# A diagonal of a 2-D prefix sum: another first load, and the corner loaded with the last batch

## Chip, cores and metric

One core of one Trainium2 chip. The metric is the device time of one execution in microseconds (us), lowest is best. Most executions of one kernel lie within 0.3% of each other.

## The reference

```python
x = randn(4, 4224, 4224)              # float32, 285.47 MB
ps = cumsum(cumsum(x, axis=1), axis=2)
diag = diagonal(ps, axis1=1, axis2=2)
return cumsum(diag, axis=1)            # (4, 4224)
```

Every element of x counts somewhere, so all of it has to be read once. For each batch the kernel sums row pieces and column pieces, and from these builds the increments of the diagonal.

## The kernel before

GpSimd's software queue loads x in strips of 768 or 384 rows and casts them to bf16 on the way, three strips ahead. VectorE, ScalarE and TensorE sum each strip. In the last batch, the last rows are split: *part a* (256 rows) and *part b* (128 rows, whose columns lie in four quarters), so that little is left to do after the last byte. One piece, the *head*, is fetched by the SP queue at the very start, while GpSimd still prepares its first descriptors.

```python
HC = 528
src_a = x[LB, T0:TB, :].rearrange("(h p) w -> p h w", p=P)
head = last.tile([P, 2, HC], FP32, name="head")
nc.sync.dma_start(out=head, in_=src_a[:, :, N - HC : N])      # corner of part a
...
for i in range(NBUF):                                          # first strips
    t = strip_tile()
    load_rows(t, 0, i * F2 * P)                                # nc.gpsimd.dma_start
...
row_sums(hs[:, 0:2], head)                                     # at the start
for h in range(2):
    masked(hmu[:, h, :w], head[:, h, HC - w : HC], um1[:, :w], hu[:, h : h + 1])
...
# last batch, after its strips: part a, then the quarters of part b
for sb, c0, c1 in ((0, 0, CB), (1, 0, CB), (2, 0, CB), (3, 0, bcut), (3, bcut, CB)):
    nc.gpsimd.dma_start(out=part_b[:, sb, c0:c1], in_=...)
...
row_sums(arows, asum)                                          # totals of part a
weigh(arows[:, 0:1], weights, 0, start=True)                   # matmuls into fin (PSUM)
weigh(arows[:, 1:2], weights, P)
weigh(ones_col, by, M0)                                        # by: quarter 0 of part b
weigh(dtot, weights, M0)
for k, ca in ((0, 512), (1, 448)):
    act_sum(bsum[:, k, 0:1], part_b[:, k + 1, :ca])
    pair_sum(bsum[:, k, 1:2], part_b[:, k + 1, ca:])
    if k == 1:
        finish(0, M0)                                          # yl = fin + c12
    row_sums(btot[:, k : k + 1], bsum[:, k])
    weigh(btot[:, k : k + 1], weights4, M0 + (k + 1) * R)
... # esum of quarter 3, three matmuls into fin_e, finish(M0, GW), ye = fin_e + yl
```

## Time and profile before

| | before |
|---|---|
| median of the first three runs | 668.09 us |
| median of the six runs beside the changed kernel | 668.83 us (667.1 to 669.88) |
| span of the profiled execution | 665.7 us |
| busy: DMA engines / VectorE / TensorE / ScalarE | all but the ends / 50% / 31% / 21% |

### The profile page before, as it was taken

How to read it: one execution, taken by the hardware profiler on the slowest of the kernel's cores; microseconds unless marked ns; L12 is line 12 of the kernel's file. 1: busy time of each engine (PE TensorE's matmuls, PEld its weight loads, DVE VectorE, ACT ScalarE, POOL GpSimd, SP SyncE). 2: the span in 40 equal slices, each digit the busy share in tenths (PEclk: the TensorE clock that was granted, in tenths of full speed). 3: DMA queues.
4: the chain of work that ended last, by engine and by line, in shares of the span. 5: the costliest groups of instructions: out<-in, count | busy, mean ns of one | idle time of the engine just before them, and what ended most of it. 6: DMA issues, size and time to landing. Idle time of an engine off the chain costs nothing.

```text
span 665.7 us, 2561 instructions
## 1 busy us (share of the span) xinstructions
PE 204.8 (31%) x979; PEld 98.2 (15%) x979; DVE 334.6 (50%) x166; ACT 140.3 (21%) x226; POOL 32.0 (5%) x61
## 2 busy tenths in 40 slices
PE   0081522403117143130221623404032264250427
PEld 0030211101003021110110311202011031120103
DVE  3161625456916153454782524436288333352867
ACT  0001121406300103040630020304063002030436
POOL 7000000000000000000000000000000000001000
PEclk9995857656558585675755957666565586766758
DMA  9999999999999999999999999999999999999998
GB/s 203 219 219 219 219 218 218 219 209 212 219 221 218 218 218 219 218 218 216 209 218 220 218 216 218 219 218 218 218 213 215 219 217 215 219 217 218 218 205 161
DMA packets 7670, 143.23 MB, mean 215 GB/s; under 512 B 702, under 2 KB 1002, under 8 KB 2154
## 3 DMA queue, kind: packets, MB, share of 16 engines
q0 software_dynamic: 7296, 142.47, 99.9%
q1 hardware_dynamic: 362, 0.61, 0.3%
q8 instruction: 7, 0.11, 0.1%
q14 instruction: 5, 0.04, 0.0%
HBM read 285.47 MB, written 0.07 MB: 429 GB/s over the span
## 4 chain that ended last, share of the span: by engine, by line
DVE 47%; another core or an unknown queue 44%; DMA 5%; PE 2%; issue 1%; DVEq 0%; POOLq 0%
DVE acc L239 29%; DVE mu L329 8%; DVE strip L330 8%; DMA strip<-in_x_dram 5%; PE d L213 1%; DVE c L445 1%; PE fold L213 1%; DVE pu L239 0%; PE fin L213 0%; DVE c L259 0%; DVE rows L369 0%; DVE acc L344 0%; PE carry_ps L213 0%; DVE carry L443 0%
## 5 line engine op out<-in xcount | busy, mean ns | idle before, releaser
L213 PE MATMUL d<-strip,sel 128*11 128x384 bf16 x603 | 138.6, 403 | 359.9 <-DMA strip<-in_x_dram 359.9
L234 ACT ACTIVATE dump<-strip 128x416 bf16<-128x416 bf16 (+8 forms) x112 | 128.4, 1146 | 521.9 <-DMA strip<-in_x_dram 519.2
L329 DVE TENSOR_TENSOR mu<-strip,um 128x4608 bf16<-128x4608 bf16 (+1 forms) x24 | 52.4, 2183 | 305.8 <-DMA strip<-in_x_dram 305.7
L239 DVE TENSOR_REDUCE acc<-strip 128x6 f32<-128x4608 bf16 (+6 forms) x23 | 196.0, 8523 | 0.8
L213 PEld LDWEIGHTS <-sel 128*11 128x11 bf16 x849 | 86.2, 102 | 504.7 <-issue 463.0
L213 PE MATMUL d<-mu,sel 128*11 128x384 bf16 x243 | 49.1, 355 | 45.8 <-DVE mu L329 45.8
L330 DVE TENSOR_TENSOR strip<-strip,mu 128x4608 bf16<-128x4608 bf16 (+1 forms) x24 | 52.4, 2183 | 1.0
L76 POOL DMA_DIRECT2D strip<-in_x_dram x24 | 16.5, 688 | 542.1 <-DVE acc L239 281.5
L234 ACT ACTIVATION_READ_ACCUMULATOR dump<-strip 128x1 f32 x112 | 20.9, 186 | 0.0
L213 PE MATMUL d<-ident,rows 128*11 128x128 f32 x24 | 5.2, 380 | 16.7 <-DVE rows L378 16.7
L213 PE MATMUL fold<-strip,ident_h 128*128 128x480 bf16 x8 | 3.4, 598 | 10.6 <-DMA strip<-in_x_dram 10.6
L213 PE MATMUL fold<-weights,quarter 32*128 32x128 f32 x2 | 0.8, 496 | 17.2 <-POOL quarter L199 17.2
L213 PE MATMUL d<-halves,rows 128*11 128x64 f32 x48 | 5.6, 299 | 0.0
L94 DVE MEMSET um<- 128x4608 bf16 (+1 forms) x2 | 4.9, 2458 | 1.1 <-issue 1.1
L213 PEld LDWEIGHTS d<-halves,rows 128*11 128x11 f32 x48 | 5.1, 136 | 1.5 <-issue 1.5
L213 PEld LDWEIGHTS d<-ident,rows 128*11 128x11 f32 x24 | 2.6, 120 | 18.4 <-DVE rows L378 17.5
L95 POOL TENSOR_SCALAR_AFFINE_SELECT um<-um 128x4608 bf16<-128x4608 bf16 (+1 forms) x2 | 5.2, 2608 | 2.4 <-DVE um L94 2.4
L239 DVE TENSOR_REDUCE pu<-d 11x1 f32<-11x384 f32 x4 | 2.2, 546 | 5.2 <-PE d L213 5.2
L445 DVE TENSOR_TENSOR_SCAN c<-ones_row,carry,c 11x384 f32<-11x384 f32 x4 | 4.0, 1006 | 0.1
L445 DVE TENSOR_TENSOR_SCAN c<-ones_row,carry,d 11x384 f32<-11x384 f32 x4 | 4.0, 1000 | 0.1
L418 POOL DMA_DIRECT2D strip<-in_x_dram x5 | 2.7, 548 | 26.4 <-DMA strip<-in_x_dram 26.4
L213 PEld LDWEIGHTS <-ident_h 128*128 128x128 bf16 x14 | 1.6, 119 | 13.8 <-issue 13.5
(90 smaller groups left out, 41.5 us busy)
## 6 DMA issues: line engine op xcount, KB each, us to landing
strip<-in_x_dram POOLq DMA_DIRECT2D x19, 6336.0 KB, 76.5
strip<-in_x_dram POOLq DMA_DIRECT2D x5, 3168.0 KB, 59.7
strip<-in_x_dram POOLq DMA_DIRECT2D x1, 1080.0 KB, 49.9
strip<-in_x_dram POOLq DMA_DIRECT2D x1, 768.0 KB, 52.8
strip<-in_x_dram POOLq DMA_DIRECT2D x3, 256.0 KB, 54.0
head<-in_x_dram SPq DMA_DIRECT2D x1, 528.0 KB, 3.7
strip<-in_x_dram POOLq DMA_DIRECT2D x1, 192.0 KB, 43.2
strip<-in_x_dram POOLq DMA_DIRECT2D x1, 64.0 KB, 28.6
```

Source lines behind the costliest of these rows:

```text
L76: nc.gpsimd.dma_start(out=o, in_=x[b, r0 : r0 + f * P, :].rearrange("(p f) w -> p f w", f=f))
L94: nc.vector.memset(um, 1.0)
L95: nc.gpsimd.affine_select(out=um, in_=um, compare_op=ALU.is_gt, fill=0.0, base=0, pattern=[[-1, f], [1, f * P]], channel_multiplier=-f,)
L213: nc.tensor.matmul(o, lhsT=lhsT, rhs=rhs, start=start, stop=False, skip_group_check=True)
L234: nc.scalar.activation(out=dump[:, :w], in_=src, func=ACT.Copy, accum_out=acc)
L239: nc.vector.reduce_sum(out=acc, in_=src, axis=AX.X)
L329: nc.vector.tensor_mul(out=mu, in0=block, in1=um)
L330: nc.vector.tensor_sub(out=block, in0=block, in1=mu)
L418: nc.gpsimd.dma_start(out=part_b[:, sb, c0:c1], in_=x[b, r0 : r0 + R, :TB].rearrange("r (k c) -> r k c", k=4)[:, :, c0:c1],)
L445: nc.vector.tensor_tensor_scan(out=c12[:, i, :], data0=ones_row, data1=src, initial=carry[:, i : i + 1], op0=ALU.mult, op1=ALU.add,)
```

## The change

The intent: the first load becomes a contiguous block (32 whole rows, the first quarter of part b) in pieces of 4224 B, more pleasant for the DMA engines than 256 scattered pieces of 2112 B. Its sum is one number for each partition, so the product "by" at the end goes away. In return the corner of part a has to be loaded by GpSimd, in the last batch. The diff, cut to its core:

```diff
-    head = last.tile([P, 2, HC], FP32, name="head")
-    nc.sync.dma_start(out=head, in_=src_a[:, :, N - HC : N])
+    head = last.tile([P, N // 4], FP32, name="head")
+    nc.sync.dma_start(
+        out=head, in_=x[LB, TB : TB + R, :].rearrange("r (k c) -> (r k) c", k=4)
+    )
 ...  # weights4 by iota, shift and max instead of a matmul (cut)
-    row_sums(hs[:, 0:2], head)
-    ...                       # masked sums of the head
+    row_sums(htot, head)
 ...
             if not whole and s == 0:      # after the first strip of the last batch
+                corner = last.tile([P, 2, HC], BF16, name="corner")
+                nc.gpsimd.dma_start(out=corner, in_=src_a[:, :, N - HC : N])
             if not whole and s == 1:
+                row_sums(hs[:, 0:2], corner)
+                ...                       # masked sums of the corner
 ...
-                (0, 0, CB),               # first quarter of part b
 ...
-        ... by_ps, by
-        weigh(arows[:, 0:1], weights, 0, start=True)
+        weigh(dtot, weights, M0, start=True)
+        weigh(htot, weights4, M0)
+        weigh(arows[:, 0:1], weights, 0)
         weigh(arows[:, 1:2], weights, P)
-        weigh(ones_col, by, M0)
-        weigh(dtot, weights, M0)
 ...
-            if k == 1:
-                finish(0, M0)
-            row_sums(btot[:, k : k + 1], bsum[:, k])
-            weigh(btot[:, k : k + 1], weights4, M0 + (k + 1) * R)
+        finish(0, M0)
+        for k in range(2):
+            for i in (1, 0):
+                weigh(bsum[:, k, i : i + 1], weights4, M0 + (k + 1) * R)
```

More of the change, by code (lines that the diff above doesn't have):

```diff
@@ L66 @@
     HC = 528
+    R = P // 4
     src_a = x[LB, T0:TB, :].rearrange("(h p) w -> p h w", p=P)
-    head = last.tile([P, 2, HC], FP32, name="head")
-    nc.sync.dma_start(out=head, in_=src_a[:, :, N - HC : N])
+    head = last.tile([P, N // 4], FP32, name="head")
+    nc.sync.dma_start(
+        out=head, in_=x[LB, TB : TB + R, :].rearrange("r (k c) -> (r k) c", k=4)
+    )
     def strip_tile():
@@ L192 @@
     )
-    R = P // 4
-    quarter = consts.tile([R, P], FP32, name="quarter")
-    nc.gpsimd.memset(quarter, 1.0)
-    for base, step in ((0, 1), (3, -1)):
-        nc.gpsimd.affine_select(
-            out=quarter,
-            in_=quarter,
-            compare_op=ALU.is_ge,
-            fill=0.0,
-            base=base,
-            pattern=[[step, P]],
-            channel_multiplier=-4 * step,
-        )
+    steps = consts.tile([P, P], I32, name="steps")
+    nc.gpsimd.iota(steps, pattern=[[4, P]], base=7, channel_multiplier=-1)
+    nc.vector.tensor_single_scalar(
+        out=steps, in_=steps, scalar=2, op=ALU.arith_shift_right
+    )
+    weights4 = consts.tile([P, P], FP32, name="weights4")
+    nc.vector.tensor_scalar_max(out=weights4, in0=steps, scalar1=0.0)
     ident_h = consts.tile([P, P], BF16, name="ident_h")
@@ L215, in matmul @@
         )
-    w4_ps = psum_s.tile([P, P], FP32, name="fold")
-    matmul(w4_ps, quarter, weights[:R, :P], start=True)
-    weights4 = consts.tile([P, P], FP32, name="weights4")
-    nc.vector.tensor_copy(out=weights4, in_=w4_ps)
-    weights4_h = consts.tile([P, P], BF16, name="weights4_h")
-    nc.vector.tensor_copy(out=weights4_h, in_=w4_ps)
-    ones_col = consts.tile([P, 1], FP32, name="ones_col")
-    nc.vector.memset(ones_col, 1.0)
     def fold_in(o, src, c0, c1, w, start=False):
@@ L284 @@
     dtot = last.tile([P, 1], FP32, name="dtot")
+    htot = last.tile([P, 1], FP32, name="htot")
     hs = last.tile([P, 3], FP32, name="hs")
@@ L287 @@
     hmu = last.tile([P, 3, GW], BF16, name="hmu")
-    row_sums(hs[:, 0:2], head)
-    for h in range(2):
-        w = GW - h * P
-        masked(hmu[:, h, :w], head[:, h, HC - w : HC], um1[:, :w], hu[:, h : h + 1])
-    nc.vector.tensor_sub(out=asum[:, :, 0], in0=hs[:, 0:2], in1=hu[:, 0:2])
+    row_sums(htot, head)
     for b in range(B):
@@ L357 @@
                 nc.gpsimd.dma_start(out=diag_b, in_=x[b, TB:N, TB:N])
+                corner = last.tile([P, 2, HC], BF16, name="corner")
+                nc.gpsimd.dma_start(out=corner, in_=src_a[:, :, N - HC : N])
             if not whole and s == 1:
                 row_sums(hs[:, 2:3], diag_b)
+                nc.vector.memset(hs[:R, 2:3], 0.0)
+                row_sums(hs[:, 0:2], corner)
+                for h in range(2):
+                    w = GW - h * P
+                    masked(
+                        hmu[:, h, :w],
+                        corner[:, h, HC - w : HC],
+                        um1[:, :w],
+                        hu[:, h : h + 1],
+                    )
+                nc.vector.tensor_sub(
+                    out=asum[:, :, 0], in0=hs[:, 0:2], in1=hu[:, 0:2]
+                )
                 masked(hmu[:, 2, :P], diag_b, um1[:, :P], hu[:, 2:3])
@@ L485, in finish @@
             )
-        by_ps = psum_s.tile([P, P], FP32, name="fold")
-        for c in range(0, CB, P):
-            matmul(by_ps, part_b[:, 0, c : c + P], weights4_h, start=c == 0)
-        by = last.tile([P, P], FP32, name="by")
-        nc.scalar.copy(out=by, in_=by_ps)
-        weigh(arows[:, 0:1], weights, 0, start=True)
+        weigh(dtot, weights, M0, start=True)
+        weigh(htot, weights4, M0)
+        weigh(arows[:, 0:1], weights, 0)
         weigh(arows[:, 1:2], weights, P)
-        weigh(ones_col, by, M0)
-        weigh(dtot, weights, M0)
         bsum = last.tile([P, 2, 2], FP32, name="bsum")
-        btot = last.tile([P, 2], FP32, name="btot")
         for k, ca in ((0, 512), (1, 448)):
```

## The prediction

> **What bounds the kernel now.** I read the page first, for what the time is made of, then the chain of waits, to see where the transfers stop setting the pace, and then the timeline of the start and of the end.
>
> The page says that the sixteen DMA engines never rest:
>
> ```profile
> DMA  9999999999999999999999999999999999999998
> q0 software_dynamic: 7296, 142.47, 99.9%
> HBM read 285.47 MB, written 0.07 MB: 429 GB/s over the span
> ```
>
> Every slice is at 9, and nearly all of it is the software queue that GpSimd feeds. The input is 4 x 4224 x 4224 x 4 bytes = 285.47 MB, so everything is read once. No engine is near that: VectorE, the busiest, has 50%. A change that reads as many bytes can therefore win or lose only where the DMA engines do not yet run (the first microseconds) and where the time after a landing is still to pay (the last ones). The end of the chain of waits shows how much that is:
>
> ```profile
> 638.16 10.59 another core or an unknown queue
> ...
> 648.80 3.36 PE fold L213 x8
> 652.15 3.58 PE d L213 x24
> ...
> 658.40 1.00 DVE c L445
> 659.41 0.60 DVE asum L239
> ...
> 660.10 0.17 DVE arows L239
> ...
> 660.32 1.85 PE fin L213 x10
> ...
> 662.19 0.04 DVE yl L483
> ...
> 662.53 0.14 DVE btot L239
> ...
> 662.72 0.27 PE fin L213 x2
> ...
> 663.03 0.45 PE fin_e L213 x6
> ...
> 663.50 0.18 DVE ye L522
> ```
>
> The wait of 10.59 us is a wait for data: at 648.8 us the last strip (rows of the last group but one) lands. From there to the last add at 663.68 us the chain never waits for data again. The stream goes on beside it, and the packet records of the trace put the last packet at 662.40 us. So two paths end together: the computing that follows the landing at 648.8, and the landing of the last block. The timeline shows the second one, and what the ten matmuls of the first are:
>
> ```profile
> 660.32 1.24 PE L213 MATMUL fin<-weights,arows 128*1 128x384 f32 x4 [0.79 <-DVE arows L239]
> 661.39 0.38 PE L213 MATMUL fin<-by,ones_col 128*1 128x128 f32 x2
> 661.61 0.38 PE L213 MATMUL fin<-weights,dtot 128*1 128x128 f32 x2
> 661.83 0.33 PE L213 MATMUL fin<-weights,btot 128*1 128x96 f32 x2
> 662.46 0.47 ACT L234 ACTIVATE dump<-strip 128x320 bf16<-128x320 bf16 x1 [0.27 <-DMA strip<-in_x_dram]
> ```
>
> The last block's sum starts at 662.46, ends with its read-out at 663.02, and fin_e starts at 663.03; the other path's last fin matmuls end at 662.99. They meet within 0.05 us. Lengthening either lengthens the kernel.
>
> At the start the load of the head is alone:
>
> ```profile
> 0.82 0.45 SPq L69 DMA_DIRECT2D head<-in_x_dram  x1
> 1.33 2.25 POOL L76 DMA_DIRECT2D strip<-in_x_dram  x3 [0.81 <-POOLq L538]
> ```
>
> In the packet records the head's 256 pieces of 2112 B run from 1.89 to 4.17 us, and the software queue's first packet starts at 3.78 us. Each engine takes its first strip packet within some 10 ns of its last head piece.
>
> **What the Trainium skill says.** "DMA: Bandwidth & Descriptors", section "Queues, rings and completion order": an engine serves its queue rows in turn, a packet at a time. In this trace the pieces of an engine's head are all done before its first strip packet; so either the strips' descriptors came just then, or they stood behind head pieces already fetched. The trace does not decide it, and what a quicker head is worth hangs on it. Same page, "Why small descriptors are slow (HBM only)": a packet has a fixed overhead. The trace agrees and gives its size: 2048 B written took 173 ns, 4320 B 340 ns, 25344 B 1886 ns, which is 22 ns + 0.0735 ns a byte. Most of the 22 ns overlaps with the next packet: in 658 to 660 us, nearly all packets of 2048 B, the engines moved 209 GB/s, against 217 in a steady stretch. Same page, "SWDGE vs HWDGE vs iDMA": only the software path casts; hence the head is fp32 from SP while the corner becomes a bf16 load by GpSimd. "PSUM — Partial Sum Buffer", section "PSUM bank collisions raise a hardware error": PSUM is to be guarded by bank and not by address. The built program agrees: see the third item below.
>
> **The change, part by part.**
>
> 1. *Head.* Both loads have the same 540,672 B: 128 pieces of 4224 B for 256 of 2112 B. Without the start-up, 16 pieces x 86 ns = 1.38 us for each engine become 8 x about 164 ns = 1.31 us (twice 86 less one fixed part of about 8 ns, an estimate). Measured is 1.96 us per engine; the 0.58 us above 1.38 is slow first pieces (up to 916 ns). If that goes with the number of pieces, or a block in one place opens faster than 256 scattered rows, half of it goes: 0.07 + 0.29 = 0.36 us at best, if the strips' descriptors are already there. I count 0.2 us for not knowing.
>
> 2. *Corner instead of the first quarter of part b.* The corner's 256 packets write 1056 B: 0.0735 x 1056 = 78 ns, and about 5 ns that does not overlap, x 256 / 16 = 1.32 us of all engines. The quarter that goes has 128 packets of 2048 B: 156 ns x 128 / 16 = 1.25 us. The stream's end moves by +0.07 us. But the corner is queued behind the first strip of the last batch, and the quarter stood behind all strips and part a. Every landing between moves back by 1.32 us: also the strip at 648.8 on which the long chain hangs.
>
> 3. *The end.* From 648.8 to the end of arows at 660.27 nothing is changed, so arows ends at 660.27 + 1.32 = 661.59. Then come two matmuls of arows (four passes, 1.24 us with their drain) instead of ten passes (1.85 us): the by product is gone, dtot and htot are weighed earlier. They are done at 662.88, and the add into yl runs to about 663.28 (0.41 us at 662.19 before). The four matmuls of bsum now stand behind this add: the program makes the first of them wait for VectorE's 150th completion, which is that add, because both touch one PSUM tile. They start at 663.33. The sums of pairs (btot) and their two waits are gone, but 96-column and 64-column matmuls come twice: by the spacing above (0.22 us for two passes of 128 columns) 2 x 0.16 + 2 x 0.11 = 0.55 us. fin_e starts at 663.88 and takes 0.45; ye starts at about 664.35 instead of 663.50. Sum: **+0.85 us**, of which +1.32 from the later landing and -0.47 from the shorter path after arows. The path by the last block gives only +0.07 and no longer counts.
>
> 4. *Beside other work.* Three DVE operations on the corner move from the start to the second strip of the last batch: 1.2 + 0.55 + 0.42 + 0.16 us, where VectorE next waits 17.04 us for data; costs nothing. The loads there have two strips queued ahead. Making weights4 by iota and shift instead of a matmul ends long before the first strip lands at 34.8 us. ACT loses a copy of 0.27 us, PE eight matmuls of 0.62 us that were hidden.
>
> Net: 0.85 - 0.2 = **+0.65 us**, 0.1%: 668.09 + 0.65 = about 668.7 us.
>
> **The rivals.** (a) *The head's gain is whole or more*: the strips' descriptors wait from about 3 us, and a block in one place starts so fast that 0.8 us are won; then the two cancel, 668.1 or somewhat less. For it speaks that all sixteen engines switch to the strip without a gap. Against: GpSimd begins its issue at 1.33, and I see no record of when descriptors are ready. (b) *The stream sets the end*: if the long chain had slack, only +0.07 and the head's gain count: 667.9. Against it stand the waits of the chain above, which meet within 0.05 us. (c) *Small pieces in mid-stream cost more*: corner packets at the full 22 ns each would be 1.6 us rather than 1.32: 669.0. (d) *GpSimd's queue runs dry* in the last batch, since two loads take completion semaphores in turn: a slice of DMA at less than 9, some microseconds. Against: one part-b load fewer, and each such wait is for a load that landed 25 us or more before the end.
>
> **Range and chances.** The three runs before span 667.1 to 669.24, so the median of three has some 0.7 us of noise; the terms add about 0.5. I take 667.2 to 670.0. Two per cent is 13 us, for which no view has room, short of a surprise in (d): 0.01 for each side.
>
> **What would show it.** Right: in the changed profile the last strip's landing is later by about 1.1 us (1.32 less the head's gain), the last packet moves by less than 0.3 us, the yl add ends near 663.1 and bsum matmuls begin just after it, with a wait on VectorE; the first strip packets begin 0 to 0.4 us earlier. Wrong: the long chain ends where it did, or the strip lands no later, which would mean that I have mis-sized either the corner or the head; or the DMA row drops in the last batch.

## The result, and the profile after

| | before | after |
|---|---|---|
| median of six runs | 668.83 us | 670.37 us (669.97 to 671.68) |
| span of the profiled execution | 665.7 us | 668.8 us |
| last strip lands (start of the work on it) | 648.80 us | 652.14 us |
| last packet of the strips' queue ends | 662.40 us | 664.46 us |
| ye starts | 663.50 us | 666.64 us |

The ratio is 1.0028 (95% interval 1.0012 to 1.0044), some 1.9 us slower. A ratio here is the mean time of one kernel's runs over that of the other's of the same rounds, so it is not quite the ratio of the medians quoted. By the rule of 2% the verdict is "same"; the time was outside my range, and the change cost about three times what I had counted. The two profiles differ by more, 3.1 us: the profiled execution of before was one of its quicker ones (667.37 us).

From the page of the changed kernel:

```profile
DMA  9999999999999999999999999999999999999996
q0 software_dynamic: 7424, 142.48, 99.6%
HBM read 285.49 MB, written 0.07 MB: 427 GB/s over the span
```

The bytes are as predicted (16 KB more read); no slice but the last, which now holds more time without transfers, is below 9. So the queue did not run dry in the last batch. The end of the chain of waits, changed kernel (start, duration, what; "another core or an unknown queue" is the view's name for a wait that it cannot put down to anything, here the one for the strip's data):

```profile
641.49 10.61 another core or an unknown queue
...
652.14 3.36 PE fold L210 x8
655.49 3.68 PE d L210 x24
...
663.54 0.17 DVE arows L227
...
663.76 1.25 PE fin L210 x4
...
665.04 0.42 DVE yl L482
...
665.50 0.73 PE fin L210 x8
...
666.25 0.29 DVE yl L482
...
666.64 0.18 DVE ye L513
```

The chain has the shape that I drew: the wait for data (10.61 us), then no more wait for data; four matmuls of arows, the add into yl, then the eight passes of bsum behind this add. From the landing to ye it takes 666.64 - 652.14 = 14.50 us, before 14.70. What is off is the landing: 3.34 us later, not 1.1. Most of this goes back to the start. What the strips' queue did from 4 to 10 us, in packets, MB and share of 16 engines (overlapping packets count twice); before:

```profile
q0 software_dynamic: 56, 1.42, 110.9%
```

and after:

```profile
q0 software_dynamic: 42, 1.06, 93.4%
```

A quarter less. The packet records show how. (The kept ones do not name a packet's engine. Engines are told apart here by which packet ends where the next one begins, which is sure near the start and less so further on.) In these records, in the changed kernel, the head is done as early as before (4.07 us, before 4.16), 13 of the engines take their first strip packet by 4.10 us, but three take it only from 5.47 us on, and 14 of the 51 strip packets that begin before 10 us last over 2.2 us (2 of 62 before; the usual is 1.89). By 10 us the stream is 0.84 us behind that of before and stays there to the end. It is worse than the mean: at 20 us the slowest engine has done 7.14 strip packets and the fastest 8.44, 2.4 us apart (before 8.23 to 8.68, 0.8 us). Each engine has its own 344 packets of 25344 B, so a late engine stays late, and a strip has landed when the last engine is done with it. At the usual 1.89 us a packet, the slowest engine is 8.23 - 7.14 = 1.09 packets, or 2.06 us, behind the slowest of before.

### The profile page after: what moved, and what is told of

It reads as the page before. It is cut to its first block, busy times and chain, and to the rows that moved or that the text cites. A ratio compares the mean times of both kernels' runs of the same rounds, so it can differ in the third digit from the quotient of the medians.

```text
span 668.8 us, 2545 instructions
## 1 busy us (share of the span) xinstructions
PE 205.5 (31%) x973; PEld 97.7 (15%) x973; DVE 335.6 (50%) x165; ACT 140.1 (21%) x225; POOL 31.5 (5%) x59
## 4 chain that ended last, share of the span: by engine, by line
DVE 47%; another core or an unknown queue 44%; DMA 5%; PE 2%; issue 1%; DVEq 0%; POOLq 0%
DVE acc L227 28%; DVE mu L314 8%; DVE strip L315 8%; DMA strip<-in_x_dram 5%; PE d L210 1%; DVE c L444 1%; PE fold L210 1%; DVE pu L227 0%; PE fin L210 0%; DVE c L247 0%; DVE rows L369 0%; DVE acc L329 0%; DVE hmu L247 0%; PE carry_ps L210 0%
## 5 line engine op out<-in xcount | busy, mean ns | idle before, releaser
L227 DVE TENSOR_REDUCE parts<-strip 128x3 f32<-128x3072 bf16 x1 | 3.4, 3354 | 0.0
```

The lines of the kernel that those rows point to most:

```text
L227: nc.vector.reduce_sum(out=acc, in_=src, axis=AX.X)
```

## The experiments

Fifteen runs were made, in four sets, each set on one chip beside the kernel before, and each with one profile. Those called wrong sum the wrong data in the last batch; the comparison with the reference does not see a fault of that size. Their outputs are wrong, which doesn't matter for the times.

**Which half of the change costs?** The kernel before with only the new head:

```diff
-    nc.sync.dma_start(out=head, in_=src_a[:, :, N - HC : N])
+    nc.sync.dma_start(
+        out=head.rearrange("p h c -> p (h c)"),
+        in_=x[LB, TB : TB + P // 4, :].rearrange("r (k c) -> (r k) c", k=4),
+    )
```

> The kernel before with nothing changed but the place that the head is read from: one block of 32 rows in 128 pieces of 4224 B (the result is wrong on purpose). Theory A, the start: in the changed kernel's trace three of the sixteen DMA engines begin their first strip packet only at about 5.5 us instead of about 4.1, and the first packets of all engines take 2 to 3 us instead of 1.9; the stream is 0.86 us behind by 10 us, the slowest engine 2 us, and never catches up. If the shape of the head causes that, this run shows the same: first packets at 5.5 us, stream behind by 0.7 to 1.0 us, and the time +0.8 to +2.0 us over before. Rival B, chance of one execution: the start is like before and the time within 0.4 us of before. Rival C, the tail alone: also no difference.

Measured: 669.49 us against 667.82, ratio 1.0026 (1.0013 to 1.0038): 1.7 us. The stream is 1.17 us behind at 10 us, four engines begin only from 5.5 us, and the last strip lands at 651.23 us, 2.43 later than before. The opposite, the changed kernel with the old head:

```diff
-        out=head, in_=x[LB, TB : TB + R, :].rearrange("r (k c) -> (r k) c", k=4)
+        out=head.rearrange("p (h c) -> p h c", h=2), in_=src_a[:, :, N - HC : N]
```

> The changed kernel with the head read from where the kernel before reads it, in 256 pieces of 2112 B (the result is wrong on purpose). Theory A: the start is as before (all engines at their first strip packet by 4.2 us), the last strip lands about 1.3 to 1.5 us later than before (the corner alone) instead of 3.35, and the time is +0.4 to +1.1 us over before. Rivals B and C: the time is as that of the changed kernel, +1.5 to +2 us, though under B the start may look either way.

Measured: 668.47 us, ratio 1.0011 (0.9998 to 1.0023): about 0.7 us; 0.18 us behind at 10 us. The strip landed at 650.96 us in this profile, 2.16 later than before rather than 1.3 to 1.5; one engine was again a packet late (7.45 at 20 us, mean 8.41). From landing to ye: 14.29 us. So the head costs, clear of noise; that the corner costs too is seen in the landing, while its time is not clear of noise. Theory B (chance of one execution) and C (the tail alone) fall.

**Were the strips' descriptors waiting?** The kernel before without a head (`- nc.sync.dma_start(out=head, ...)`, `+ nc.vector.memset(head, 0.0)`):

> The kernel before without any load of the head (its tile is set to zero by VectorE; the result is wrong on purpose). It shows when the strips' descriptors are ready with no other load ahead. If they are ready early (theory of the change: the head fills time that the queue needs anyway), first strip packets begin between 2.5 and 3.5 us and the stream is 0.5 to 1.0 us ahead of before: time -0.5 to -1.0 us. If instead descriptors come engine by engine at 3.5 to 5.5 us whatever the head is, first packets spread over that stretch here too and the time is +0.3 to +1.5 us over before.

Measured: 667.33 us, ratio 0.9993 (0.9981 to 1.0006). All sixteen engines begin their first strip packet between 2.84 and 3.44 us: descriptors are usable at 2.84 us here, when with a head its pieces are still under way. But these first packets last 2.5 to 3.3 us; the second ones are at 1.89. So a first packet that starts cold loses about 0.8 us, and of the early start only 0.21 us is left. The head in the kernel before is nearly hidden, as the change supposed: without its 0.54 MB (1.26 us at the mean 429 GB/s of the page) the profiled stream gains 0.21 us and the time 0.5, which is not clear of noise.

**The add between the matmuls.** The changed kernel with one add instead of two (`- finish(0, M0)`, and at the end `finish(0, GW)` for `finish(M0, GW)`):

> The changed kernel with one add into yl over all 384 columns at the end instead of two, so that the matmuls of bsum need not wait for the first add (the result is right). My account of the tail: after arows the changed kernel needs 2.88 us to the start of ye; here the matmuls follow one another (1.1 + 0.55 + 0.35 us) and one add of about 0.5 us follows, so ye starts about 2.4 us after arows: -0.4 to -0.5 us against the changed kernel. Rival: the last block's arrival sets the end, then less than 0.1 us changes.

> The changed kernel with the old head and with one add into yl at the end (the result is wrong on purpose, for the head). The run with one add alone gained nothing measurable, but its profiled execution had half the clock granted to TensorE in the last 4 us. If the wait for the first add is worth what I counted, this is 0.3 to 0.5 us under the run with the old head alone, so about +0.3 us over before (ratio 1.0002 to 1.0006); if the wait is hidden, 1.0011 again.

Measured: with the new head 669.97 us, ratio 1.0031 (1.0018 to 1.0045), no gain against 1.0028 and 1.0025 for the changed kernel; with the old head 669.33 us, ratio 1.0005 (0.9988 to 1.0021), where 1.0011 is inside the interval. Unsettled. In both profiles TensorE had half the clock at this very place. Run with one add, then the changed kernel (columns: stretch, length, then busy time of TensorE, weight loads, VectorE, ScalarE, GpSimd, then granted clock, share of DMA, GB/s):

```profile
663.60:666.60 3.00, 3.00 (x12) 1.24 (x13) 1.27 (x8) 1.45 (x6) 0.00 (x0) 0.50 0.07 12
```

```profile
663.80:666.80 3.00, 2.09 (x18) 0.97 (x18) 2.00 (x11) 1.17 (x4) 0.00 (x0) 1.00 0.05 10
```

At 0.50 the four passes of arows took 2.29 us, at 1.00 they took 1.24. The Trainium skill says, in "TensorE: Matmul & The Clock Gate", Part 1, that the clock falls to half when the engine has had little to do and is released by activity. The trace agrees as far as the two values go. It was at half in the tail of six of the fifteen profiled executions and at full in that of before and after, so one profile of these kernels' ends can be 1 us off for this reason alone. From landing to ye those six took 15.29 to 16.08 us, all others 14.18 to 14.70. Each of the six was also the slowest execution of its kernel (without a head 668.92 us, the other four 667.2 to 667.36), so a part of the spread in the times may be this clock; the executions without a profile do not show it.

**Size of the pieces or their lying together?** The kernel before with 128 scattered pieces of 4224 B (`in_=x[LB, T0 : T0 + P, 0 : 2 * HC]`), run twice:

> The kernel before with a head of 128 pieces of 4224 B that lie in 128 different rows (the start of each of the first 128 rows of part a; the result is wrong on purpose). It tells the size of the pieces from their lying together. If fewer and larger pieces make the start slow: several engines begin their first strip packet after 5.2 us, the stream is behind before by 0.8 to 1.2 us at 10 us, and the time is +1 to +2 us over before, as with the block. If it is the lying together: start as before, all engines by 4.3 us, behind by less than 0.3 us, time within 0.5 us of before.

> Once more the kernel before with 128 scattered pieces of 4224 B. The first time its profiled execution had the slow start (1.3 us behind), but its times averaged 1.0001 with a spread of 4 us on a chip where before itself spread over 2.7 us. If size alone counts, ratio 1.0015 to 1.003 as with the block of 4224-B pieces (1.0026); if only size and lying together do, 0.9995 to 1.0005.

and with the block in 256 pieces of 2112 B:

```diff
+        in_=x[LB, TB : TB + P // 4, :].rearrange(
+            "r (k c) -> (r k) c", k=8
+        ).rearrange("(h p) c -> p h c", p=P),
```

> The kernel before with a head that reads the block of 32 rows in 256 pieces of 2112 B, the same number and size as before (the result is wrong on purpose). The other half of the same question: if size and number of the pieces count, start and time as before (within 0.5 us); if it is the lying together, the stream is 0.8 to 1.2 us behind at 10 us and the time +1 to +2 us over before.

Measured: scattered large pieces 1.0001 (0.9981 to 1.0021) and, again, 1.0024 (1.0005 to 1.0042), with the slow start in both profiles (1.30 and 0.74 us behind). The block in small pieces 0.9988 (0.9972 to 1.0003), 0.01 us behind, all engines started by 4.15 us. So where the pieces lie does not count, as far as these three profiles show. The times of the scattered run do not agree well with each other, so that verdict rests on the profiles and on the second run.

**The change with small pieces, and the change again.** The changed kernel, its block in 256 pieces; a gap in the tile keeps neighbours from being joined into one (right result):

```diff
-    head = last.tile([P, N // 4], FP32, name="head")
+    head = last.tile([P, 2, HC + 16], FP32, name="head")
-        out=head, in_=x[LB, TB : TB + R, :].rearrange("r (k c) -> (r k) c", k=4)
+        out=head[:, :, :HC],
+        in_=x[LB, TB : TB + R, :].rearrange("r (k c) -> (r k) c", k=8).rearrange(
+            "(p h) c -> p h c", h=2
+        ),
```

> The changed kernel whole (right result), only that the block of 32 rows is fetched in 256 pieces of 2112 B: a gap in the tile keeps two neighbouring pieces from being joined. If the size of the pieces is what costs the start: all engines at their first strip packet by 4.3 us, the stream less than 0.5 us behind, and the time about 1 us under the changed kernel of this same set, so +0.4 to +1.1 us over before (ratio 1.0006 to 1.0016). If not: as the changed kernel, ratio about 1.003.

> The changed kernel itself once more, on the chip of the other three, as the measure for them: ratio 1.002 to 1.004, three or more engines at their first strip packet only after 5.2 us.

Measured on the same chip: 668.95 us, ratio 1.0009 (0.9992 to 1.0025), against 670.27 us, ratio 1.0025 (1.001 to 1.0039). With small pieces all engines start by 4.53 us and the stream is 0.17 us behind at 10 us. The difference of the ratios, 0.0016 or 1.1 us, is what the 128 large pieces cost in the whole change; the intervals of the ratios overlap, but the difference of the two sets of six times, 1.07 us with a standard error of 0.33, is clear of noise. The strips' queue from 4 to 10 us, small pieces, then the change as it is:

```profile
q0 software_dynamic: 53, 1.34, 106.2%
```

```profile
q0 software_dynamic: 38, 0.96, 88.2%
```

**Where the corner stands in the queue.** The changed kernel with the old head, and with the corner's 256 pieces behind part a, where nothing uses them (wrong):

```diff
-                nc.gpsimd.dma_start(out=corner, in_=src_a[:, :, N - HC : N])
+                nc.gpsimd.memset(corner, 0.0)
 ...             # after the loads of part a, into an unused part of the strip
+            spare = strip[:, 3, : 2 * HC].rearrange("p (h c) -> p h c", h=2)
+            nc.gpsimd.dma_start(out=spare, in_=src_a[:, :, N - HC : N])
```

> The changed kernel with the old head, and with the corner's 256 pieces queued behind part a instead of ahead of the last batch's strips (nothing uses them, the corner's tile is zero; the result is wrong on purpose). The same bytes, but behind the landing that the long chain hangs on. My account: the last strip lands as in before, within 0.3 us apart from the start, the chain from the landing to ye is 0.4 us shorter than before (it was 14.29 us with the corner early and the old head, 14.70 before), and the arrival of the last block sets the end: time within 0.4 us of before, and 0.5 to 1 us under the run with the old head and the corner early (ratio 1.0011). Rival: the place of the corner does not count, then it is as that run, about 1.001.

> Once more the corner behind part a, with the old head (wrong on purpose), to be held against the changed kernel with 2112-B pieces on the same chip, which has the corner ahead of the strips. If the place of the corner costs what I counted, this is 0.5 to 1.0 us under that run and within 0.4 us of before; if not, the two are alike.

Measured: 1.0003 (0.9983 to 1.0022) and 0.9998 (0.9979 to 1.0018): as before, where the two runs with the corner early and a good head had 1.0009 and 1.0011. The intervals overlap, so the times do not decide it; what does is the chain, one execution of each. The profile of the first run with the corner late does not serve for it: TensorE had half the clock in its tail, and one engine was late (7.12 packets at 20 us, mean 8.28), so that the strip was worked on only from 651.36 us. That is later than with the corner early, and against what I expected. With the corner early (change with small pieces) it starts at a landing of 650.95 us:

```profile
640.31 10.60 another core or an unknown queue
...
650.95 3.36 PE fold L213 x8
...
665.40 0.18 DVE ye L518
```

With the corner late (second run) the strip is worked on from 649.55 us, and the chain does not go back to it at all; it goes back to the last block of part b, as in the second path that I named:

```profile
619.87 43.26 DMA strip<-in_x_dram
...
663.15 0.66 DVE pair L236 x4
...
664.22 0.18 DVE ye L515
```

So in these two profiles the same bytes cost about 1.2 us less when they stand behind the landing that the chain hangs on (ye at 664.22 against 665.40). The late corner is no kernel to keep: the corner's matmuls have to be in before the increments are finished.

**Size or number?** A larger piece also means fewer of them: 8 for each engine instead of 16. Three more heads of the kernel before tell that apart: half the head (128 pieces of 2112 B, `out=head[:, 0:1, :]`), the block in 512 pieces of 1056 B, and 256 pieces of 3120 B (`HL = 780`, 258 KB more read).

> The kernel before with only half of the head, 128 scattered pieces of 2112 B (the other half is set to zero; the result is wrong on purpose). It tells number from size: with 128 pieces of 4224 B the stream was 0.74 to 1.39 us behind before at 10 us in six of six profiles, with 256 of 2112 B at most 0.42 in seven of seven. If eight pieces for each engine are too few to last until the strips start, this is slow as well: several engines' first strip packet after 5 us or first packets of 2.3 to 3 us, the stream 0.3 us or more behind, and the time +0.3 to +1.5 us over before. If the size of a piece counts, the first strip packets start at about 3.0 to 3.6 us, and the stream is level with or ahead of before by up to 0.6 us: time 0 to -0.6 us.

> The kernel before with the block of 32 rows in 512 pieces of 1056 B (the result is wrong on purpose). If smaller pieces or more of them start the stream better, it is as quick as before or up to 0.5 us quicker, no strip packet of the first 10 us above 2.3 us; if 2112 B is merely below a bound, as before within 0.3 us.

> The kernel before with 256 scattered pieces of 3120 B: as many pieces as before, half as large again; right result, 258 KB more read (0.6 us of stream). If the size counts, first strip packets of 2.3 to 3 us and the stream 0.5 us or more behind what the later end of the head explains (the head itself ends about 0.7 us later), time +1.2 to +2.5 us; if the number counts, no slow packets, time +0.4 to +0.8 us.

The packet records of all heads; "slow" are strip packets begun before 10 us that last over 2.2 us, "behind" is the lag of the strips' stream against before at 10 us:

| head | for each engine | profiles | head ends, us | slow | behind, us |
|---|---|---|---|---|---|
| 128 x 4224 B | 8 | 6 | 4.07 to 4.20 | 14 to 21 | 0.74 to 1.39 |
| 256 x 2112 B | 16 | 7 with before | 4.14 to 4.49 | 1 to 6 | 0 to 0.42 |
| 512 x 1056 B | 32 | 1 | 4.57 | 0 | 0.18 |
| 256 x 3120 B | 16 | 1 | 5.02 | 0 | 0.61 |
| 128 x 2112 B | 8 | 1 | 3.20 | 13 | -0.08 |
| none | 0 | 1 | - | 16 | -0.21 |

Times: half the head 1.0007 (0.9992 to 1.0022), 512 pieces 1.0003 (0.9989 to 1.0017), 256 larger pieces 1.0018 (1.0004 to 1.0031). With 256 larger pieces not one packet is slow, and the 0.61 us behind goes with the later end of the head (5.02 against 4.16). That speaks for the number: with 8 pieces or none, many packets are slow, with 16 or 32 few.

It is not settled, though. The half head met its first expectation in the slow packets (2.3 to 2.9 us), and three engines stood idle for 1.25 to 1.8 us after their last piece. In its first starts (13 of 16 engines by 3.52 us) and in its lag it met the second, because it also ends 1 us earlier. The 256 larger pieces cost 1.2 us, which was the forecast for the size (1.2 to 2.5), not for the number (0.4 to 0.8); the interval, 0.3 to 2.1 us, holds both, and its profile is of its quickest execution by far (667.9 us, the others 669.48 to 669.69). And in three of the seven profiles with 256 pieces of 2112 B one engine, too, took its first strip packet only at 4.99, 5.18 or 5.71 us. That 128 pieces of 4224 B start the stream badly is shown; that it is their number fits every row of the table but is not shown beyond that, and why, no run shows.

## Why the prediction was wrong, point by point

- *What bounds the kernel.* Held. The stream sets the pace, the chain after the last strip sets the end, and the last block is close behind: with the corner late it became the bound.
- *Step 1, the head: the step that failed.* I counted a gain of 0.2 us, "0.36 us at best". Measured is a loss of 1.1 us (change with large against small pieces) to 1.7 us (head alone), and 2.06 us by the slowest engine in the profile. I sized the head by its own end, and that was nearly right: engines had it by 3.55 to 4.07 us, up to 0.2 us earlier. What I left out is how the strips start behind it. Behind the 128 large pieces three engines were idle until 5.5 us and packets took 2.2 to 3.1 us, although descriptors were usable at 2.84 us in the run without a head. I also reckoned the lag as a mean, where the landing goes by the slowest engine.
- *Step 2, the corner.* Held in kind: the corner's place moves the landing, as the second run with the late corner shows. The landing moved by 3.34 us in the profile: 1.32 for the corner as predicted, and 2.06 for the slowest engine, make 3.38. The same sum, the slowest engine's lag at 20 us and 1.32 us where the corner comes early, is within 0.7 us of the landing in fourteen of the fifteen runs, and 1.2 us short in the other (scattered pieces, again). That the stream's end would move by under 0.3 us was wrong for the same reason: it moved by 2.06.
- *Step 3, the end.* Held in order but for the last link (before ye came the second add into yl, 0.29 us, and not fin_e as I had drawn), and a little too good in size: I said that the path gets 0.47 us shorter, in the profiles it got 0.20 (14.70 to 14.50), and 0.41 with the old head. bsum's first matmul started 0.46 us after the add did, as its wait on that add requires. Step 3 with step 2, +0.85 us, is what the change costs without its new head: 1.0009 and 1.0011, 0.6 to 0.7 us, though both intervals reach below 1.
- *Step 4, the hidden work.* Held. The corner's sums ran at 574.9 to 577.1 us in the second strip of the last batch, within VectorE's idle time.
- *Rivals.* (a) went the opposite way, though its premise, descriptors that wait from about 3 us, held in the run without a head. (b) is excluded by the chain of after. (d) did not occur. (c) is excluded by the packets of after: a corner packet is recorded at 100 ns, but the engine's next packet starts 82 ns after it on average (256 packets), and 16 x 82 = 1.31 us for each engine, where I had counted 1.32.
- *Range.* I took a gain or nothing from the head for granted and put no weight on a start that is worse. The sum, redone with the head's measured +1.1 in place of -0.2, is 0.85 + 1.1 = 1.95 us, against 1.9 measured; part of this agreement is built in, as the 1.1 was itself read from the whole change.

No version here beats the kernel before clearly: the best, 0.9988, sums the wrong rows and its interval reaches 1.0003.

## What to carry to other kernels

A load that fills the gap at the start is to be judged by when every engine is at full speed on the next load, not by its own end: read the packets of the first 10 us, engine by engine, because a lag there is kept to the end. Before moving bytes in a queue that sets the pace, find the landing on which the last chain hangs; here bytes ahead of it cost in full, and bytes behind it next to nothing. Where two paths end together, shortening one by half a microsecond showed nothing in the time here. And before two profiles of an end are compared, look whether TensorE had the same clock in both.

## What the Trainium skill lacked or had wrong

- "DMA: Bandwidth & Descriptors", "Queues, rings and completion order", has an engine take its queues in turn, a packet at a time, and its packet is some 9 to 17 descriptors as a rule. No page says what one record of the trace is in these terms. With no head, strip packets started at 2.84 us; with the head of before, no engine took one before its last head piece, at 3.78 us at the earliest. The 16 pieces that an engine has of the head may have been one turn, so this neither agrees nor disagrees with the page.
- The same page, "Why small descriptors are slow (HBM only)", gives each packet a fixed overhead. The traces agree (22 ns for each packet, mostly hidden), but for a load that leads in another queue this was not what counted: 128 pieces of 4224 B left the stream 0.74 to 1.39 us behind at 10 us, 256 of 2112 B at most 0.42. No page has this.
- No page tells what the first packets of a cold queue cost: 2.5 to 3.3 us where 1.89 us is usual, for 25344 B written.
- No page gives a size for how far the engines stand apart in one long stream: 0.24 to 1.44 packets of 25344 B, or some 0.5 to 2.7 us, between the first and the last of sixteen at 20 us.
